# Rewriting a hybrid decoder layer so that attention, mLSTM and cross attention are emitted between the dense projections

## Chip, cores, metric

One Trainium2 chip, all 8 cores. Each core computes one of eight batch elements; nothing is exchanged between cores. The metric is device time in microseconds (us) of the slowest core.

In the calls of the experiments, 11 of 12 fast executions of the kernel before took 3553 to 3564 us, a spread of 0.3%; the twelfth took 3604. Other executions were in a slower state, in which the cores of one die (0 to 3, or 4 to 7) show a lower granted TensorE clock than the others: one of the kernel before took 3843 us, with a mean clock of 0.83 on one die and 0.91 on the other. No slow execution was profiled. Where a profile was taken on one core, the text names it if it matters.

Engine names: PE is TensorE (matmul), PEld its weight load, DVE is VectorE, ACT is ScalarE, POOL is GpSimd, SP is the sync engine, whose queue issues most loads and stores here. In these programs every matmul writes a bank of PSUM; to evacuate a bank is to move its result on to SBUF, the on-chip memory, so that the program can use the bank again. Tile names in the views: `bk` is a PSUM bank, `mv`, `mg` and `mb` are a chunk's values, gates and decays, `Cf` is the recurrent state of the mLSTM, `hmt` its output after the root, `Pa` the exponentials of attention, `hb` the inputs of the merge.

## The reference, cut to what matters

```python
# B=8, S=2048, D=2048; weights and shapes cut
def reference(x, mem, positions, ...):
    h = rms_norm(x, norm)
    proj = h @ w_in            # qk 2048, v 1024, o 1024, z 1024, gates i,f; cq 512, ckv 512, kr 64, az 1024; c_q 1024, c_z 1024; merge gates 3*2048
    # A: mLSTM, 4 heads of 256
    qk = silu(causal_depthwise_conv(m_qk, conv_w, conv_b))       # 4 taps
    hm = mlstm_chunkwise(q, k, v, ig, lf)                        # recurrent over chunks
    hm = rms_norm(hm) * sigmoid(m_o) * silu(m_z)
    # B: latent attention, 8 heads, causal, rotary part from cos/sin of the positions
    ha = causal_block_attention(qa, ka, v_a) * silu(a_z)
    # C: cross attention, 4 heads of 256, 256 memory tokens
    hc = memory_attention(c_q, k_mem, v_mem) * silu(c_z)
    # merge
    merged = sigmoid(g_m) * (hm @ w_br_m) + sigmoid(g_a) * (ha @ w_br_a) + sigmoid(g_c) * (hc @ w_br_c)
    return rms_norm(x + merged @ w_out, final_norm)
```

## The kernel before

It runs stage after stage, with barriers between: input projections, memory projections, cross attention, latent attention, mLSTM, then twice (for each half of the tokens) merge and output. A helper inserts every semaphore wait from declared reads and writes; each engine then takes its own instructions in the order in which the program emitted them. The two mLSTM parts:

```python
# mLSTM, two heads at a time; everything of a head is loaded once for all 16 chunks
fw.dma("sp", Brs[i]..., BHv[h:h + 1, :].partition_broadcast(128), ...)   # cumulated log decays, 1 MB once per head
fw.op("act", ... EBs = exp(Brs));  fw.op("dve", ... BMs = Brs + Mneg)    # whole rows, once
def P1a(c): ...   # scores q.k of chunk c, decay weights DT = exp(BM + At), PT = scores * DT, weighted keys kw
def P1b(c): ...   # state update Cf = decay * Cf + kw.v through a PSUM bank; bf16 copy Cb
def P2a(c): ...   # output bank = qe.Cb + PT.v
def P2b(c, bos):  # normalisation: 2 DVE and 2 ACT operations
    ...tensor_scalar(max 1, *EPS) ; scalar_tensor_tensor(...)            # DVE
    activation(Ln) ; activation(Exp, scale=-0.5)                         # ACT: x ** -0.5
    ...
P1a(0); P1b(0); P1a(1); P1b(1)
for c in range(16):
    if c + 2 < 16: P1a(c + 2)
    # (cut)
```

In the qk projection a block of 2048 tokens is evacuated to SBUF, then convolved with four long DVE operations, and its SiLU is one ACT operation.

The softmax here doesn't subtract the row's maximum and nothing guards it: scores larger than these inputs give would overflow.

## Time and profile before

| | before |
|---|---|
| median, first 3 runs | 3566.68 us (3559.03 to 4069.53, the last one slow) |
| profiled execution, slowest core (6) | 3566.3 us |

The first lines of the profile page of the kernel before: the span, busy time by engine, and, in 40 equal slices of the span, the busy tenths of PE and DVE and the granted TensorE clock in tenths.

```profile
span 3566.3 us, 43630 instructions; the slowest of 8 cores (3506.5 to 3566.3 us)
PE 2956.1 (83%) x14733; PEld 1383.4 (39%) x14733; DVE 912.9 (26%) x1781; ACT 847.2 (24%) x1783; POOL 272.9 (8%) x374
PE   1899999899999993667772524799999779999978
DVE  2556333311000450422222524011111221111113
PEclk9999999999999996978885555899999889999989
```

PE is full in the projections and in merge and output, and starved from slice 16 to slice 25 (counted from 1): memory projections, the two attentions and the mLSTM, each alone. In the mLSTM (slices 22 to 25) PE is 2 to 5 tenths busy and its clock is 0.5.

The windows view of the kernel before gives sums for a stretch; columns are the window, its length, then busy us (and instruction count) of PE, PEld, DVE, ACT, POOL, then the granted clock, the DMA share, GB/s. The lines are attention, the mLSTM of two heads, and part of the merge.

```profile
1545.00:1900.00 355.00, 265.93 (x1785) 129.98 (x1783) 78.31 (x365) 180.89 (x340) 4.75 (x16) 0.85 0.21 53
1900.00:2060.00 160.00, 61.62 (x340) 34.80 (x340) 66.14 (x188) 66.29 (x224) 25.28 (x60) 0.50 0.30 93
2262.00:2755.00 493.00, 492.48 (x2272) 222.60 (x2270) 62.43 (x95) 51.02 (x94) 94.03 (x92) 1.00 0.41 84
```

The merge is at its limit: 492 of 493 us busy at clock 1.00. The mLSTM of all four heads takes 315 us (1900 to 2215) for about 123 us of PE at a granted clock of 0.50.

### The profile page before, as it was taken

Reading aid. Unit: us, or ns where it says so; the run is one execution under the profiler, and the core shown is the slowest. Engines: PE = TensorE matmul, PEld = TensorE weight load, DVE = VectorE, ACT = ScalarE, POOL = GpSimd, SP = SyncE. Lnnn points to the kernel's source line nnn. Section 1 sums busy time; section 2 is a strip of 40 time slices with the busy share of each in tenths; the row PEclk is TensorE's granted clock in tenths of the full one; section 3 lists DMA queues with packets and bytes.
Section 4 is the critical chain, followed back from the end, with each engine's and each line's share of the span. In section 5 each row is a group of like instructions: output and inputs, shape, how many; then the busy total and the mean of one; then the engine's idle time right before and its main releaser. Section 6 shows DMA issues by size and latency. Waiting matters only on the chain.

```text
span 3566.3 us, 43630 instructions; the slowest of 8 cores (3506.5 to 3566.3 us)
## 1 busy us (share of the span) xinstructions
PE 2956.1 (83%) x14733; PEld 1383.4 (39%) x14733; DVE 912.9 (26%) x1781; ACT 847.2 (24%) x1783; POOL 272.9 (8%) x374
## 2 busy tenths in 40 slices
PE   1899999899999993667772524799999779999978
PEld 1444444444444442333331212344444334444433
DVE  2556333311000450422222524011111221111113
ACT  3432211232101121445552524001110110101111
POOL 0000000000000000000001111021222002221100
PEclk9999999999999996978885555899999889999989
DMA  8542330313232247332214051644434763333633
GB/s 211 177 92 68 86 74 21 68 25 61 65 80 54 71 129 181 110 89 66 66 39 125 20 170 43 144 80 80 80 73 88 180 219 77 70 71 76 127 95 142
DMA packets 139608, 338.15 MB, mean 95 GB/s; under 512 B 42048, under 2 KB 91520, under 8 KB 124160
## 3 DMA queue, kind: packets, MB, share of 16 engines
q0 software_dynamic: 15264, 143.24, 22.1%
q1 hardware_dynamic: 124128, 192.13, 16.7%
q8 instruction: 124, 2.03, 0.2%
q14 instruction: 92, 0.75, 0.1%
HBM read 396.47 MB, written 82.08 MB: 134 GB/s over the span
## 4 chain that ended last, share of the span: by engine, by line
PE 75%; DMA 8%; ACT 5%; issue 4%; DVE 4%; SPq 2%; another core or an unknown queue 0%; DVEq 0%; POOL 0%; ACTq 0%; POOLq 0%
PE bk L315 20%; PE bk L1018 18%; PE bk L304 13%; PE bk L1023 9%; PE bk L1062 6%; SPq L93 2%; PE bk L761 2%; ACT sb_Pa L746 2%; DMA sb_wpo<-wOUT 2%; DMA sb_hb<-HMT 2%; PE bk L741 1%; PE bk L743 1%; DMA sb_rn_xt<-mem 1%; DMA sb_rn_xt<-x 1%; ACT sb_rn_junk L234 1%
## 5 line engine op out<-in xcount | busy, mean ns | idle before, releaser
L1018 PE MATMUL bk<-sb_hTh,sb_wpg 128*128 128x512 bf16 x3072 | 682.8, 381 | 36.5 <-DMA sb_wpg<-wG 25.4
L315 PE MATMUL bk<-sb_wpA,sb_hT 128*128 128x512 bf16 (+1 forms) x3328 | 687.5, 367 | 8.2 <-DVE sb_stA L471 8.2
L1018 PEld LDWEIGHTS bk<-sb_hTh,sb_wpg 128*128 128x128 bf16 x3072 | 301.4, 98 | 402.3 <-issue 42.7
L315 PEld LDWEIGHTS bk<-sb_wpA,sb_hT 128*128 128x128 bf16 x3328 | 309.6, 99 | 373.0 <-issue 34.1
L1023 PE MATMUL bk<-sb_hb,sb_wpb 128*128 128x512 bf16 x1536 | 351.1, 382 | 26.4 <-DMA sb_hb<-HMT 26.4
L304 PE MATMUL bk<-sb_hT,sb_wpA 128*128 128x512 bf16 (+1 forms) x1664 | 367.9, 385 | 2.3 <-issue 2.3
L1029 ACT ACTIVATE sb_sg<-bk 128x512 f32<-128x512 f32 x192 | 104.2, 595 | 900.2 <-PE bk L1018 871.5
L304 PEld LDWEIGHTS bk<-sb_hT,sb_wpA 128*128 128x128 bf16 (+1 forms) x1664 | 166.1, 100 | 203.3 <-issue 23.9
L1023 PEld LDWEIGHTS bk<-sb_hb,sb_wpb 128*128 128x128 bf16 x1536 | 151.1, 98 | 211.1 <-issue 32.6
L1035 DVE TENSOR_TENSOR sb_tmpc<-sb_sg,bk 128x512 f32<-128x512 f32 x128 | 82.4, 684 | 576.5 <-PE bk L1023 576.5
L746 ACT ACTIVATE sb_Pa<-bk 128x512 bf16<-128x512 f32 (+1 forms) x320 | 169.8, 533 | 155.6 <-PE bk L761 54.3
L761 PE MATMUL bk<-sb_vx,sb_Pa 128*128 128x129 bf16 x1088 | 126.3, 237 | 53.4 <-DVE sb_Pa L748 28.1
L1062 PE MATMUL bk<-sb_wpo,sb_mergedT 128*128 128x512 bf16 x512 | 121.8, 398 | 33.0 <-DMA sb_wpo<-wOUT 33.0
L761 PEld LDWEIGHTS bk<-sb_vx,sb_Pa 128*128 128x128 bf16 x1088 | 80.3, 105 | 167.7 <-issue 160.0
L257 PE MATMUL bk<-sb_identb,sb_rn_xb 128*128 128x128 bf16 x288 | 33.6, 309 | 134.6 <-DVE sb_rn_xb L246 134.6
L741 PE MATMUL bk<-sb_qn,sb_kn 128*128 128x512 bf16 (+1 forms) x320 | 126.8, 396 | 16.8 <-DMA sb_kn<-KNT 15.8
L1031 DVE TENSOR_TENSOR sb_acc<-sb_sg,bk 128x512 f32<-128x512 f32 x64 | 44.0, 688 | 360.4 <-PE bk L1023 356.7
L743 PE MATMUL bk<-sb_qr,sb_kr 128*128 128x512 bf16 (+1 forms) x320 | 127.2, 398 | 0.0
L1038 POOL TENSOR_TENSOR sb_acc<-sb_acc,sb_tmpc 128x512 f32<-128x512 f32 x64 | 80.7, 1261 | 601.8 <-DVE sb_tmpc L1035 597.2
L1062 PE MATMUL bk<-sb_wpoa,sb_mergedT 128*128 128x512 bf16 x512 | 118.9, 393 | 8.0 <-POOL sb_mergedT L1041 8.0
L876 PE MATMUL bk<-sb_mqT,sb_mkT 128*128 128x128 bf16 x128 | 25.2, 300 | 119.7 <-DMA sb_mkT<-MKT 74.7
L531 DVE CAST sb_ob<-bk 128x512 bf16<-128x512 f32 x48 | 32.9, 689 | 349.1 <-ACT sb_ob L529 345.0
(227 smaller groups left out, 2408.4 us busy)
## 6 DMA issues: line engine op xcount, KB each, us to landing
sb_wpg<-wG POOLq DMA_DIRECT2D x32, 1536.0 KB, 10.4
sb_wpA<-wA POOLq DMA_DIRECT2D x18, 2048.0 KB, 16.1
sb_wpb<-wBR POOLq DMA_DIRECT2D x32, 768.0 KB, 13.5
sb_rn_xt<-x SPq DMA_DIRECT2D x16, 1024.0 KB, 6.6
sb_xo<-x SPq DMA_DIRECT2D x16, 1024.0 KB, 7.8
out<-sb_xo SPq DMA_DIRECT2D x16, 1024.0 KB, 4.8
HT<-sb_hT SPq DMA_DIRECT2D x16, 512.0 KB, 2.7
sb_wpM<-wMEM POOLq DMA_DIRECT2D x4, 2048.0 KB, 21.0
```

The lines of the kernel that those rows point to most:

```text
L304: fw.op("pe", lambda e: e.matmul(bk[0:M, 0:n], lhsT=wv[:, kc, c0:c0 + M], rhs=src[:, kc, tb * 512:tb * 512 + n], start=(kc == 0), stop=(kc ...
L315: fw.op("pe", lambda e: e.matmul(bk[:, 0:ncols], lhsT=src[:, kc, tt * 128:(tt + 1) * 128], rhs=wv[:, kc, 0:ncols], start=(kc == 0), stop=( ...
L741: fw.op("pe", lambda e: e.matmul(bs[:, 0:ncols], lhsT=kn[:, kc_], rhs=qn[:, q0:q0 + ncols], start=True, stop=False), reads=[r_kn, r_qn], w ...
L743: fw.op("pe", lambda e: e.matmul(bs[:, 0:ncols], lhsT=kr[:, kc_], rhs=qr[:, q0:q0 + ncols], start=False, stop=True), reads=[r_kr, r_qr], w ...
L746: fw.op("act", lambda e: e.activation(out=P[:, 0:ncols], in_=bs[:, 0:ncols], func=AF.Exp, scale=SC), reads=[r_bs], writes=[r_P])
L761: fw.op("pe", lambda e: e.matmul(bo[:, 0:129], lhsT=P[:, j * 128:(j + 1) * 128], rhs=vx[:, kt, 0:129], start=(kt == 0), stop=(kt == qt)), ...
L1018: fw.op("pe", lambda e: e.matmul(gb[tb][0][:, 0:512], lhsT=wgv[:, kc, b * 128:(b + 1) * 128], rhs=hTh[:, kc, tb * 512:(tb + 1) * 512], sta ...
L1023: fw.op("pe", lambda e: e.matmul(rb[tb][0][:, 0:512], lhsT=wbv[:, kc, b * 128:(b + 1) * 128], rhs=hbs[b][:, kc, tb * 512:(tb + 1) * 512], ...
L1029: fw.op("act", lambda e: e.activation(out=sg[:], in_=gb[tb][0][:, 0:512], func=AF.Sigmoid), reads=[gb[tb][1]], writes=[r_sg])
L1035: fw.op("dve", lambda e: e.tensor_tensor(out=tmp[:], in0=sg[:], in1=rb[tb][0][:, 0:512], op=ALU.mult), reads=[r_sg, rb[tb][1]], writes=[r_ ...
L1038: fw.op("pool", lambda e: e.tensor_tensor(out=acc[:, tc_], in0=acc[:, tc_], in1=tmp[:], op=ALU.add), reads=[r_tmp, r_acc], writes=[r_acc])
L1062: fw.op("pe", lambda e: e.matmul(bk[:, 0:512], lhsT=mergedT[:, kc, t8 * 128:(t8 + 1) * 128], rhs=wov[:, kc, 0:512], start=(kc == 0), stop= ...
```

## The change

The intent: give PE dense matmuls while attention, mLSTM and cross attention wait. The program is rewritten around Python generators. `dense_all` yields after each piece of projection; a scheduler then advances the current side job as long as its estimated PE work is below 0.36 of the dense work. Latent attention goes beside the az, qk and v projections and the beginning of oz, the mLSTM beside cq/cz, cross attention beside the first seven gate units of the merge. The diff has 2,400 lines; its core (all cuts marked):

```diff
+        sides = [(mla_gen, "MLA", 0.36), (mlstm_gen, "ML", 0.36), (c_gen, "CC", 0.36)]
+        for v in dense_all():
+            ...
+            st["d"] += v
+            while st["s"] < st["ratio"] * st["d"] and side_step():
+                pass
@@ PSUM: dense work has two banks, the side job six
+            misc, bub, bob = Ring(SB[0:2]), Ring(SB[2:4]), Ring(SB[4:6])
@@ attention, feature-major: up to 512 columns a matmul, softmax sums on DVE, reciprocal through DRAM
-    matmul(bo[:, 0:129], lhsT=P[:, j*128:(j+1)*128], rhs=vx[:, kt, 0:129])        # one per query tile
+    mm(po, (…, slice(512 - n, 512)), vx[:, kt, :], p[:, 0:n])
+    tt("dve", acc[:, o:512], acc[:, o:512], p[:, 0:n], ALU.add)
@@ convolution of one 512-token bank at a time, gate by tanh
+    copy("act", p[:, 3:515], bk[:, 0:512])
+    ts("dve", y, p[:, 3:515], cw[3], cb) ; 3 x stt("dve", y, p[:, tap:tap + 512], cw[tap], y)
-    activation(out=ob, in_=ybuf, func=AF.Silu)
+    act(th, y, AF.Tanh, scale=0.5) ; stt("dve", o, th, 1.0, y, ALU.add, ALU.mult) ; store
@@ mLSTM: all four heads a chunk, decays loaded chunk by chunk, root by Newton steps on DVE
+    B2s = tiles("mb", 2, [128, 4, 128], F32)
+    def loads1(c): mv, mg, and  dma(B2s[c % 2], BHv[:, chunk c].partition_broadcast(128))
+    def P1a(c): act(EB, B2, Exp) ; tt("dve", BM, B2, Mneg) ; ... DT = exp(BM), PT, kw
+    def rsqrt(y, x, t): shift, subtract, 3 x (mult, mult, mult-add, mult)          # DVE, [128, 2]
+    for c in range(16):
+        P1a(c + 1) ; P1b(c, 4 heads) ; P2(c, 0) ; P2(c, 1) ; tail(c - 1)
+        loads1(c + 2)
@@ tables for the rotary part: full width, one quarter of the tokens in one go, in the c_q projection
@@ one output phase at the end (before: twice merge then output)
```

## The prediction

> **What bounds it now.** TensorE. The engine table gives PE 2956 of 3566 us busy; the chain of waits is 75% PE. A dense 128x512 matmul starts every 215.9 ns (chain of waits: 32 in 6.91 us) at a granted clock of 1.00 (windows view): dense stages are at their limit. Counted in such matmuls, the program is about 12,400, 2680 us. In the other 890 us PE waits or runs slow. By stage (windows view; PE work my count):
>
> - start, norm of x: 120 us, PE 30 busy
> - input projections: 1226 for about 1185
> - memory projections and cross attention: 199 for 65
> - attention: 355 for 176; PE waits for ACT's exp (533 ns mean) and DVE's mask
> - mLSTM: 315 for 64, granted clock 0.50
> - merge and output: 1351 for 1216, with 135 of waits for hb, wOUT and first weights at stage edges
>
> [...] all eight cores hold 1.00 in the merge.
>
> **What changes.** Attention goes beside the az, qk, v and oz projections, mLSTM beside cq/cz, cross attention beside seven prepaid gate units. PE work falls little: feature-major attention replaces 1088 x 129 columns by 320 matmuls of up to 512, rope projections shrink (UQ 384 to 256, KR 128 to 64). My count is 12,270 matmuls, 2650 us, plus 30 for float32 denominators. Barriers, the hT round trip and the second output-weight load go. [...]
>
> **What stays or is added** (estimates from durations in the groups view):
>
> - Start: x arrives at 3.4 to 5 us a tile; PE fills from 40 us: 55.
> - Trig on DVE (about 10 us a quarter), uq weights: 20.
> - Memory projections stay exposed: four 2 MB loads at 16 to 21 us through two buffers against 7 us of matmul each: 45.
> - qk with attention is DVE-bound: per unit one 0.38 and four 0.684 us operations, plus 1.9 us of softmax sums, masks and scaling, 5.1 against 4.7 us of PE: 35 over 64 units.
> - Attention denominators: PE waits for DVE sum, then reciprocal, 32 times about 1.5 us: 45.
> - mLSTM: DVE about 16.5 us a chunk (two reciprocal roots, each 14 dependent 0.165 us operations) against 15 of PE, and only two output banks: 65.
> - Cross attention partly runs alone, then hb2 and branch weights load: 35.
> - Tail: 10.
>
> 2680 + 310 = 2990; some waits overlap, so I say **2960 us, 2850 to 3080** (8 in 10). Faster by over 2% 0.97, within 2% 0.02, slower 0.01.
>
> **What would show it.** PE busy above 90%; granted clock near 1.00 during mLSTM; no slice with PE at 2 to 5 tenths after the start except the memory projections (waiting for wMEM) and the cross-attention tail; DVE over 90% busy in the qk stretch, PE waits there and in mLSTM released by DVE; the merge still 10.4 us per gate-branch unit, without 30 us gaps for hb or wOUT; dense matmuls still 215.9 ns apart.
>
> **What would make it wrong.** [...] An in-order DVE or SP queue, waiting on the reciprocal's DRAM round trip, could hold back evacuations. If interleaving hides DVE chains better than I think, 2850.

(Three passages, two on the granted clock and one on the tables of ACT, are cut from the prediction, since they rested on no trace or run of this case. No term of the sum goes with them: it came to 2680 us of PE work, 2650 plus 30, and 310 of waits, 2990 in all, put at 2960 for overlap. What was measured: in the merge of the kernel before, from 2400 to 2600 us, all eight cores were granted 1.00. The kernel after shows no table load on ACT from 509 to 1573 us, with tanh and exponentials side by side in the qk stretch; a table load takes 1.28 us there. The 30 us for float32 denominators were an estimate; the 256 matmuls for them were busy 37 us in the kernel after.)

## The result

| | before | after |
|---|---|---|
| median | 3571.99 us (4 runs) | 3721.02 us (4 runs, 3692.53 to 3993.81) |
| ratio of fast runs | 1 | 1.0375 (95%: 1.0331 to 1.0419) |
| control, another chip | 3559 to 3563 us | 3625.18 us, its only fast run |

A ratio is the mean time of one kernel's fast runs over that of the other's fast runs of the same rounds, so it is not quite the ratio of the medians.

The kernel is slower. In the two runs behind the 1.0375, cores 6 and 7 ended at 3686 to 3700 us with a clock of 0.89, while the other six ended at 3597 to 3629 us with 0.90 to 0.91. They count as fast, but in the control no core of the fast run ended after 3625 us, and all clocks were 0.90 to 0.91. I take 3625 us, 1.018 of the control's fast before runs, as the undisturbed size, and use the control for sums by stage. Either way the predicted 2960 us is missed by over 660 us.

The answering lines of the page of the kernel after (core 6, the late one), with the first line of its chain of waits, which names what the chain that ended last consisted of:

```profile
span 3699.6 us, 41439 instructions; the slowest of 8 cores (3597.0 to 3699.6 us)
PE 2875.4 (78%) x13618; PEld 1367.3 (37%) x13885; DVE 1295.0 (35%) x2738; ACT 761.1 (21%) x1509; POOL 341.2 (9%) x410
PE   3679569877779999944444446748999999999998
DVE  3535214567674455423333333131111111111143
PEclk9889789989899999977777678969999999999999
PE 60%; DMA 15%; DVE 13%; issue 6%; ACT 4%; SPq 2%; DVEq 1%; ACTq 0%; POOLq 0%
```

The hole of before has not closed. From slice 18 to slice 24 PE is 4 tenths busy at 0.6 to 0.7 clock, although dense work was available all that time. The chain of waits went from 75% PE and 8% DMA to 60% PE and 15% DMA.

The windows view of the kernel after, the same core: start, qk with attention, cq/cz with mLSTM, the end of cross attention, part of the merge.

```profile
0.00:280.00 280.00, 159.07 (x890) 82.31 (x906) 109.24 (x143) 117.87 (x257) 5.10 (x13) 0.85 0.33 90
660.00:1128.00 468.00, 353.67 (x1523) 163.00 (x1553) 321.15 (x602) 124.93 (x252) 2.64 (x5) 0.89 0.24 62
1570.00:2287.00 717.00, 318.80 (x1492) 152.01 (x1520) 245.75 (x888) 139.37 (x325) 36.32 (x33) 0.72 0.25 53
2330.00:2520.00 190.00, 112.42 (x524) 47.70 (x533) 52.43 (x101) 27.19 (x47) 11.00 (x18) 0.75 0.69 159
2520.00:2962.00 442.00, 439.86 (x2004) 199.87 (x2044) 62.55 (x91) 48.95 (x82) 120.60 (x147) 1.00 0.50 83
```

The merge is as full as before. In the mLSTM stretch of 717 us no engine is busy for half the time. So it is not a matter of work but of waiting. The waits view of that stretch (engine, instruction, what it waited for: us in total, times, longest):

```profile
PE bk L289 <- DVE Cf_13317 L309: 280.7, 57, 23.5
DVE BM_127_13307 L302 <- DMA mb_121_13301<-BH: 133.1, 8, 29.0
DVE BM_127_13307 L302 <- DMA mb_122_13302<-BH: 123.0, 8, 19.1
```

PE waited 281 us for the state update on DVE. DVE waited 256 us, 16 us in each of 16 chunks, for one load: `mb`, the decays of the chunk, broadcast to all partitions. One chunk in the timeline of the kernel after (start us, duration, engine, instruction, in brackets the idle time before it and what ended it):

```profile
1908.74 0.44 SPq L132 DMA_DIRECT2D mb_121_13301<-BH  x1
...
1922.38 0.69 DVE L302 TENSOR_TENSOR BM_127_13307<-mb_121_13301,Mneg_13243 128x512 f32<-128x512 f32 x1 [15.32 <-DMA mb_121_13301<-BH]
1923.14 2.46 POOL L302 TENSOR_TENSOR qe_134_13314<-mq_111_13291,EB_126_13306 128x512 bf16<-128x512 bf16 x2 [42.22 <-ACT EB_126_13306 L293]
...
1928.11 0.37 PE L289 MATMUL bk<-mv_116_13296,kw_136_13316 128*128 128x257 bf16 x1 [18.79 <-DVE Cf_13317 L309]
```

The load is issued at 1908.74, behind those of `mv` and `mg`. Its data is there at 1922.4. The very next DVE instruction of the program reads it. The reason is in the loop: `loads1(c + 2)` stands at the end of iteration c, and iteration c + 1 begins with `P1a(c + 2)`. Nothing lies between. The buffer had been free for nearly two chunks, since only `P1a(c)`, at the start of iteration c - 1, reads it (in this trace at 1827.8); the place in the program alone makes the load late. DVE and ACT stand at it for 15.3 and 18.3 us, and the evacuation of a dense bank, which is emitted later, stands behind it: the last matmuls into that bank ended at 1909.1, but it was first read at 1924.95. PE had by then used both banks of the state update for two matmuls at 1908.93; the next one needs a bank that DVE has to free, and PE stops for 18.8 us. The next load of `mb` is issued at 1952.5, so a chunk took 44 us.

### The profile page after: what moved, and what is told of

The parts are those of the page before. It is cut to its first block, busy times and chain, and to the rows that moved or that the text cites. A ratio compares the mean times of both kernels' runs of the same rounds, so it can differ in the third digit from the quotient of the medians.

```text
span 3699.6 us, 41439 instructions; the slowest of 8 cores (3597.0 to 3699.6 us)
## 1 busy us (share of the span) xinstructions
PE 2875.4 (78%) x13618; PEld 1367.3 (37%) x13885; DVE 1295.0 (35%) x2738; ACT 761.1 (21%) x1509; POOL 341.2 (9%) x410
## 4 chain that ended last, share of the span: by engine, by line
PE 60%; DMA 15%; DVE 13%; issue 6%; ACT 4%; SPq 2%; DVEq 1%; ACTq 0%; POOLq 0%
PE bk L289 59%; DMA mb_122_13302<-BH 4%; DMA mb_121_13301<-BH 3%; DVE y_100_5053 L309 2%; DVE y_101_5054 L309 2%; SPq L132 2%; DMA hb_193_19251<-HCT 1%; DVE den_80_3545 L302 1%; DMA xt_14_61<-x 1%; DMA xo_209_26268<-x 1%; DMA cq_170_18127<-CQT 1%; DVE Cf_13317 L309 1%; DVEq L71 1%; DMA RDC<-rtc_184_18141 1%; ACT DT_128_13308 L293 1%
## 5 line engine op out<-in xcount | busy, mean ns | idle before, releaser
L289 PE MATMUL bk<-hT_10_52,w_12_54 128*128 128x512 bf16 x622 | 180.2, 440 | 4.3 <-issue 2.4
L289 PE MATMUL bk<-hT_9_51,w_11_53 128*128 128x512 bf16 x657 | 173.5, 415 | 11.5 <-DMA w_11_53<-wA 7.7
L289 PE MATMUL bk<-hT_10_52,w_11_53 128*128 128x512 bf16 x653 | 168.1, 406 | 3.6 <-DVE e_3_47_3200 L309 1.9
L289 PE MATMUL bk<-hT_9_51,w_12_54 128*128 128x512 bf16 x623 | 162.2, 406 | 1.2 <-issue 0.4
L289 PE MATMUL bk<-w_11_53,hT_9_51 128*128 128x512 bf16 (+1 forms) x630 | 132.5, 363 | 19.0 <-ACT hT_9_51 L297 6.7
L289 PE MATMUL bk<-w_11_53,hT_10_52 128*128 128x512 bf16 (+1 forms) x629 | 134.6, 367 | 5.2 <-ACT hT_10_52 L297 4.8
L289 PE MATMUL bk<-hT_9_51,wg_153_18094 128*128 128x512 bf16 x503 | 116.4, 386 | 8.4 <-DMA wg_153_18094<-wGB 7.9
L289 PE MATMUL bk<-hT_9_51,wg_155_18096 128*128 128x512 bf16 x502 | 112.9, 379 | 0.5
L289 PE MATMUL bk<-hT_9_51,wg_154_18095 128*128 128x512 bf16 x502 | 112.8, 379 | 0.5
L289 PE MATMUL bk<-hT_10_52,wg_155_18096 128*128 128x512 bf16 x502 | 112.6, 379 | 0.5
L289 PE MATMUL bk<-hT_10_52,wg_154_18095 128*128 128x512 bf16 x502 | 112.4, 379 | 0.5
L289 PE MATMUL bk<-hT_10_52,wg_153_18094 128*128 128x512 bf16 x502 | 112.4, 379 | 0.5
L289 PE MATMUL bk<-w_12_54,hT_9_51 128*128 128x512 bf16 (+1 forms) x501 | 110.5, 365 | 0.7 <-issue 0.2
L289 PE MATMUL bk<-w_12_54,hT_10_52 128*128 128x512 bf16 (+1 forms) x503 | 109.0, 362 | 0.4
L309 DVE SCALAR_TENSOR_TENSOR tm_198_19257<-sg_158_18099,bk 128x512 f32<-128x512 f32 x31 | 21.3, 687 | 246.8 <-PE bk L289 246.8
L289 PEld LDWEIGHTS bk<-hT_9_51,w_11_53 128*128 128x128 bf16 x672 | 70.1, 105 | 97.1 <-issue 35.6
L309 DVE SCALAR_TENSOR_TENSOR tm_198_19257<-sg_156_18097,bk 128x512 f32<-128x512 f32 x30 | 20.6, 688 | 239.4 <-PE bk L289 239.4
L289 PEld LDWEIGHTS bk<-hT_10_52,w_12_54 128*128 128x128 bf16 x640 | 70.6, 111 | 89.6 <-issue 38.0
L289 PEld LDWEIGHTS bk<-hT_10_52,w_11_53 128*128 128x128 bf16 x672 | 69.1, 103 | 85.9 <-issue 19.7
L293 ACT ACTIVATE sg_156_18097<-bk 128x512 f32<-128x512 f32 x46 | 27.5, 597 | 342.0 <-PE bk L289 342.0
L289 PEld LDWEIGHTS bk<-hT_9_51,w_12_54 128*128 128x128 bf16 x640 | 65.6, 104 | 77.1 <-issue 17.8
L289 PEld LDWEIGHTS bk<-w_11_53,hT_9_51 128*128 128x128 bf16 x640 | 63.7, 100 | 81.3 <-issue 28.0
```

Of the source, the lines that this page charges most:

```text
L289: fw.op("pe", lambda e: e.matmul(bk[o] if not isinstance(o, bass.AP) else o, lhsT=lhsT, rhs=rhs, start=start, stop=stop), reads=reads, wri ...
L293: fw.op("act", lambda e: e.activation(out=out, in_=in_, func=func, **kw), reads=reads, writes=writes, accs=accs)
L309: fw.op("dve", lambda e: e.scalar_tensor_tensor(out=out, in0=in0, scalar=sc, in1=in1, op0=op0, op1=op1), reads=reads, writes=writes, accs= ...
```

## The experiments

My theory A after reading the trace: the just-in-time load, passed on by in-order engines, is the largest loss, and smaller losses of the same kind (a wait at the head of an in-order list) account for most of the rest. Rivals: B, too few PSUM banks; C, interleaving itself costs more than it brings; D, the DVE has too much work. (The expectations use letters of their own in places: "theory C" in e3_conv and e4_serial is the in-order coupling, which here belongs to A; "rival E" in e4_serial is C here; rival B of e1_mb and e6_mbring takes in the DVE's chain of operations.) Eleven runs, all correct; one of them is the unchanged kernel as a control. Sums by stage are taken from the timeline, as the time between the first stores of successive stages: the qk stretch from the first store of q to that of v, the mLSTM stretch from the first store of cq to that of `RDC` (the reciprocals of cross attention). The control ran on another chip than e1_mb to e4_serial.

### e1_mb and e2_ring: the load, or the banks

```diff
# e1_mb: a third buffer, and the load issued one chunk earlier
-B2s = tiles("mb", 2, ...)            # loaded in loads1(c), c % 2
+B2s = tiles("mb", 3, ...)            # loadsB(c), c % 3
+                loadsB(c + 3)         # after loads1(c + 2)
# e2_ring: four banks shared instead of two and two
-misc, bub, bob = Ring(SB[0:2]), Ring(SB[2:4]), Ring(SB[4:6])
+misc, bub = Ring(SB[0:2]), Ring(SB[2:6]); bob = bub
```

> The changed kernel with one thing different: the row-broadcast load of the decay sums (mb<-BH) has a third buffer and is issued one whole chunk earlier; everything else is as changed. Theory A (the mLSTM stretch, 717 us on core 6, is set by this load, issued right before the DVE and ACT instructions that need it, some 14 to 19 us of wait in each of 16 chunks, and everything behind them on the in-order DVE waits too): the stretch falls by 240 to 300 us to about 440, the kernel to about 3440 us (ratio to before 0.96 to 0.975). Rival B (the stretch is set by the DVE chain of the reciprocal roots and the two output banks): the wait only changes its name; less than 80 us gained, ratio above 1.015.

> The changed kernel with one thing different: in mLSTM, the two banks of the state update and the two banks of the output form one ring of four, so that the second pair of heads need not wait for the first pair's root chain; the load of the decay sums stays just in time. Theory A: the waits of PE for these banks (about 75 us for hmt and part of those for Cf) shrink, the load's wait stays: 60 to 110 us gained, ratio 1.01 to 1.02. Rival B: the larger part of the stretch's excess of about 360 us goes, over 200 us, ratio below 0.985.

Measured: e1_mb 3479.84 us median, fast runs 3477 to 3480, ratio 0.9754 (0.9671 to 0.9837). One load issued a chunk earlier makes the rewrite faster than the kernel before, though the interval doesn't clear 2%, so the verdict on record is "unclear". (By the order of reads the third buffer would not even be needed for that; without it nothing was run.) The mLSTM stretch fell from 713 us (control) to 559: 154 us, nearly twice what rival B allowed, but well short of the 240 to 300 that theory A had expected. e2_ring: 3604.40 us, ratio 1.0087 (0.9989 to 1.0186), stretch 665 us: 48 us, below theory A's 60 to 110 and far from rival B's 200. In e2_ring the waits for the load are all still there. The waits views of the mLSTM stretches, first of the control, then of e2_ring, then of e1_mb:

```profile
PE bk L289 <- DVE Cf L309: 220.3, 56, 18.8
DVE BM L302 <- DMA mb<-BH: 190.6, 16, 29.1
PE bk L289 <- DVE hmt L309: 76.8, 17, 6.2
```

```profile
DVE BM L302 <- DMA mb<-BH: 193.6, 16, 29.6
PE bk L289 <- DVE Cf L309: 151.4, 35, 20.2
```

```profile
PE bk L289 <- DVE hmt L309: 78.8, 17, 6.0
PE bk L289 <- DVE Cf L309: 58.9, 56, 6.8
```

In e1_mb the load does not appear among the leading waits (2 waits of DVE, 25 us in all, are left), and PE's wait for `Cf` fell from 220 us (control) to 59. The wait for `hmt` stayed as it was, 77 us before and 79 after, and now leads. Theory A holds for the largest single part, not for the size it had claimed; banks alone explain at most 48 us.

### e3_conv: order in the qk unit

```diff
-act(th, y, AF.Tanh, scale=0.5); stt("dve", o, th, 1.0, y, ...); store
+def fin_(...): act(th, ...); stt(o, ...); store
+if cfin[0] is not None: cfin[0]()      # the unit before
+cfin[0] = fin_
```

> The changed kernel with one thing different: in the qk projection the tanh, the final product and the store of a unit are emitted behind the convolution of the next unit, instead of right behind their own. Theory C (the qk stretch, 468 us for 301 us of PE work, is a coupling of two in-order queues: ACT waits for the convolution on DVE with the softmax exponentials queued behind it, and DVE then waits for the tanh): 60 to 110 us gained, ratio 1.01 to 1.022. Rival D (DVE is simply full there): under 25 us, ratio 1.03 or more.

Here it is ACT's order that counts. Its tanh waits for DVE's four convolution operations (4.22 us below), and the exponentials of attention, emitted later, stand behind the tanh. From the timeline of the kernel after in the qk stretch, and from the waits view of ACT there (the first of six such lines, 299 us in all):

```profile
809.76 2.46 DVE L309 SCALAR_TENSOR_TENSOR y_100_5053<-pre_97_5050,cw_5044,y_100_5053 128x512 f32<-128x512 f32 x3
812.32 0.63 ACT L293 ACTIVATE e_2_52_3205<-y_100_5053 128x512 f32<-128x512 f32 x1 [4.22 <-DVE y_100_5053 L309]
813.13 0.69 DVE L309 SCALAR_TENSOR_TENSOR e_2_46_3199<-e_2_52_3205,y_100_5053 128x512 bf16<-128x512 f32 x1 [0.90 <-ACT e_2_52_3205 L293]
```

```profile
ACT e_2_52_3205 L293 <- DVE y_100_5053 L309: 57.9, 11, 10.9
```

Measured: 3588.73 us median of 5, two of them slow; fast 3565 to 3589; ratio 1.0018 (0.9924 to 1.0112), a little better than the range that the coupling had been given. The qk stretch fell from 444 us (control) to 384, with the same operations in it. ACT's wait for `y`, control first, then e3_conv:

```profile
ACT e L293 <- DVE y L309: 291.9, 63, 8.3
```

```profile
ACT e L293 <- DVE y L309: 61.1, 37, 4.0
```

PE's waits for `Pa` fell with it, from 86 to 38 us. Emitting three instructions later was worth 60 us, the lower end of the 60 to 110 expected.

### e4_serial: is interleaving a loss?

```diff
-sides = [(mla_gen, "MLA", 0.36), (mlstm_gen, "ML", 0.36), (c_gen, "CC", 0.36)]
+sides = [(mla_gen, "MLA", 1e6), (mlstm_gen, "ML", 1e6), (c_gen, "CC", 1e6)]
```

> The changed kernel with the interleaving off: each of the three side programs is emitted in one piece when its inputs are ready (the ratio of side to dense work set to a million). Theory A and C (the interleaving itself helps, what costs are single waits within it): slower than the changed kernel by 60 to 250 us, ratio 1.055 to 1.11. Rival E (putting small work between the dense matmuls, with two banks left to the dense ones, is what costs): faster than the changed kernel by 50 us or more, ratio below 1.02.

Measured: 3748.92 and 3752.61 us (the median of 3890 us holds two slow runs), 1.052 of the fast before runs, just under the range expected. Interleaving is a gain of some 125 us over the whole, so rival C falls as stated. By stage it is split, though. At the first oz store interleaving is 172 us ahead (1287 us against 1459), but there the serial kernel is done with attention (last store at 1022 us), while the interleaved one still carries the end of it through oz (to 1521). The fair mark is the first store of `BH`, with which the mLSTM begins: 1579 against 1679, a gain of 101 us with latent attention. From there to the start of cross attention, the mLSTM with its projections, interleaving gains only 13 us (712 against 724). With one late load per chunk, overlapping the two was worth hardly more than running them after one another. The serial run also shows the new mLSTM by itself, in the windows view, and below it, from the waits view, how long DVE waited for the load of `mb` there:

```profile
1691.00:2130.00 439.00, 112.23 (x630) 68.39 (x630) 216.20 (x752) 108.94 (x263) 34.77 (x30) 0.53 0.27 54
```

```profile
DVE BM L302 <- DMA mb<-BH: 80.9, 8, 28.9
```

439 us alone, where that of the kernel before took 315. DVE waited 81 us of it for the same load, in 8 of the 16 chunks (191 us in all 16 in the control). Even less these 81 us (an estimate: 358) it is the slower of the two: the rewrite brought a slower mLSTM and counted on hiding it. Alone and without the late load it was not run.

### e5_control, e6_mbring, e7_all, e8_best

```diff
# e6_mbring = e1_mb + e2_ring
# e7_all    = e6 + e3_conv + two more:
#   tables: the operations of a quarter go into a list; five of them after each projection unit
-                        trig_step()          # a whole quarter, after each of the first four c_q units
+                    trig_step(5)
#   cross attention: side work at 0.8 instead of 0.36 of dense work, hb loads ahead of the seven gate units
# e8_best   = e7 + one root for all four heads of a chunk, 11 DVE operations instead of 2 x 17
-rsqrt(sc[:, 8:10], ...)   twice a chunk, three Newton steps of 4 operations
+2 Newton steps of 3:  u = y*y ; u = u*x ; y = (u - 3) * y ; then (u - 12) * y    # constants folded into the scale
```

> The changed kernel again, untouched, as the control of this call. Expected 3610 to 3720 us, 1.015 to 1.04 of the kernel before. In its first runs two cores of one die (6 and 7) ended at 3690 us while the other six ended at 3597 to 3629 us: if that was a state of that chip or of that run, this one comes out near 3620 us; if it belongs to the kernel (cores 6 and 7 always late), near 3700 us.

> The broadcast load one chunk earlier AND a four-bank ring shared by state update and output. Theory A (in the changed kernel the load hid the two-bank ring: the ring alone gave nothing because DVE and ScalarE stood at the load): with the load out of the way the ring is worth something, about 60 us: the mLSTM stretch about 500 us, the total about 3420 us, ratio 0.955 to 0.97. Rival B (with the load early, the stretch is held by the DVE's in-order list itself, whatever the number of banks): no more than the early load alone, 3470 to 3490 us, ratio 0.975, and the waits of TensorE for the state copies simply move to another tile.

> Five repairs together: load early, four-bank ring, gate of each qk unit behind the next convolution, the sine and cosine work spread five operations at a time, and cross attention with its loads ahead of its gate units and at 0.8 instead of 0.36 of side work to dense work. If the losses add up: about 3210 us, ratio 0.895 to 0.915. Rival: the losses hide behind each other, since the later stages wait for the stage before on the same DVE, and less than half of the sum arrives: 3300 us or more.

> The five repairs and a shorter reciprocal square root of the mLSTM output: one for all four heads of a chunk with two Newton steps, about 10 dependent DVE operations a chunk in place of two chains of 17. At the 0.267 us from start to start that such operations showed this saves about 6 us of DVE a chunk. Theory A (the DVE's in-order list is what holds the mLSTM stretch once the load is early): the stretch is 16 x 5 to 6 us = 80 to 95 us shorter than with the five repairs, total about 3120 us. Rival B (the stretch is held by TensorE or by loads): under 20 us less.

| run | fast runs, us | ratio (95%) | to first kr store | qk | cq/cz with mLSTM | cross attention to end |
|---|---|---|---|---|---|---|
| e5_control | 3625.18 | 1.018, one run | 293 | 444 | 713 | 1334 |
| e6_mbring | 3442 to 3472 | 0.9691 (0.963 to 0.9751) | 293 | 446 | 523 | 1368 |
| e7_all | 3342 to 3345 | 0.9389 (0.937 to 0.9407) | 260 | 383 | 524 | 1329 |
| e8_best | 3254 to 3260 | 0.9145 (0.9124 to 0.9166) | 258 | 382 | 445 | 1324 |

The columns of a row come from its profiled run; that of e6_mbring (3471.66 us) was the slowest of its fast ones, its last column above that of the others.

In e6_mbring the ring is worth 36 us in its stretch after the load was moved (559 to 523 us), against 48 us before; in total ratio it brings 0.6%. The ratio is inside theory A's range, at its upper end; the stretch gained 36 us where about 60 had been expected. So the ring is worth something with the load early, but not more than with it late: that the load had hidden the ring's worth, as the expectation said, is not borne out. Rival B's "no more than the early load alone" falls (3442 to 3472 us against e1_mb's 3477 to 3480).

In e7_all the gains of stages add up: 33 (start) + 61 (qk) + 189 (mLSTM) + 5 (cross attention to end) = 288 us, where the profiled spans of control and e7 differ by 283 us (3624.1 to 3341.4). But the total of 3343 us misses the expected 3210; it lies in the range that the rival had named (3300 or more), though the rival's reason, losses that hide behind each other, is not what the sums show: more than half of the expected gain arrived, and the single gains had been set too high. Of the two parts not tried alone, spreading the table work brought 33 us, and the cross-attention repair 5 us, in the sum of its stretch to the end. The waits views of PE up to the first kr store, control first, then e7_all, show the table work: in the control PE stands behind whole quarters of up to 12.5 us, since a projection's evacuation waits behind them on DVE.

```profile
PE bk L525 <- DVE c L309: 50.3, 5, 12.5
```

```profile
PE bk L525 <- DVE c L309: 19.9, 9, 3.2
```

In e8_best the mLSTM stretch falls by 79 us, 4.9 us in each of 16 chunks, with 23 DVE operations a chunk fewer. That is just under the 80 to 95 us expected; the total misses the expected 3120 by as much as e7_all had missed its own. The windows views of the stretch, e7_all first, then e8_best:

```profile
1489.00:2012.00 523.00, 342.31 (x1727) 164.78 (x1726) 267.74 (x889) 144.00 (x338) 38.28 (x35) 0.83 0.37 90
```

```profile
1490.00:1935.00 445.00, 323.35 (x1696) 161.65 (x1729) 198.23 (x522) 145.50 (x338) 38.91 (x35) 0.86 0.45 106
```

The operations are tiny, [128, 2]. Four of them in the timeline of the kernel after:

```profile
1901.48 0.17 DVE L320 TENSOR_SCALAR stm_150_13330<-stm_150_13330 128x2 int32<-128x2 int32 x1
...
1901.76 0.17 DVE L321 TENSOR_SCALAR stm_150_13330<-stm_150_13330 128x2 int32<-128x2 int32 x1
...
1902.03 0.16 DVE L323 TENSOR_TENSOR stm_150_13330<-stm_150_13330 128x2 f32<-128x2 f32 x1
...
1902.30 0.16 DVE L324 TENSOR_TENSOR stm_150_13330<-stm_150_13330 128x2 f32<-128x2 f32 x1
```

Each lasts 0.165 us, but they start 0.27 us apart. 23 x 0.27 = 6.2 us of DVE a chunk, of which 4.9 arrived. (The root now also comes once, after all four heads; that change of order is in the 4.9 too.) Planning with the duration alone, as the prediction did, undercounts such a chain by 40%.

### e9_order, e10_tap, e11_last

```diff
# e9_order, on e8_best: mq/mk loads one chunk earlier; reciprocal's load one step later
-                if c % 2 == 1 and c // 2 + 2 < 8: loads(c // 2 + 2)
+                if c % 2 == 0 and c // 2 + 2 < 8: loads(c // 2 + 2)
-                dma(rb, RDC ...)      # right after the store to RDC
+                rbl[0] = rbl_         # issued in the next step, behind its loads
# e10_tap, on e8_best: first convolution tap on ACT, from the bank
-ts("dve", y, p[:, 3:515], cw[3], cb, mult, add)
+act(y, bk[:, 0:512], AF.Identity, scale=cw[3], bias=cb)
# e11_last = e9 + e10 + softmax sums on POOL
-tt("dve", acc[:, o:512], acc[:, o:512], p[:, 0:n], ALU.add)
+tt("pool", ...)
```

> The kernel of e8_best with two changes of the order in which loads are given to the queue, no work added or removed. In the mLSTM the loads of q and k for the next pair of chunks are issued one chunk earlier (their buffers are free by then). In cross attention the load that brings the reciprocals back is issued one step later, behind the loads of the next step, because in e8_best the queue stood 64 us for 16 such round trips and the next step's cq came late (PE waited 38 us for mk and 38 us for cq there). Theory: each wait shows in its own stretch: mLSTM 445 to about 415 us, cross attention 134 to about 110 us, total 3200 to 3215 us against 3254. Rival (TensorE would have waited for the next thing in those places): under 15 us in all.

> The kernel of e8_best with the first tap of the convolution of the qk stretch on ScalarE (scale and bias read from the bank), 64 operations of about 0.57 us off the DVE. Theory (the qk stretch, 382 us in e8_best, is held by the DVE, busy 306 us of it, TensorE work in it 321 us at a clock of 0.91): DVE falls by about 35 us, the stretch by 20 to 35 us, to about 350 us. Rival (it is held by the order of hand-overs between ScalarE and DVE): no gain, 375 us or more, since a hand-over is added.

> All repairs together: e9_order, e10_tap, and the adds of the softmax sums that are still on the DVE given to POOL where the tile is a whole one. If gains of different stretches add: about 3160 us, 0.885 to 0.895 of the kernel before. The adds on POOL alone are open: by the DVE theory they bring the qk stretch 10 to 25 us further down than e10_tap; the rival is that POOL is slower for such an add and TensorE waits for the sums instead, then the stretch is as long as in e10_tap or longer.

| run | fast runs, us | ratio (95%) | qk | cq/cz with mLSTM | cross attention to merge loads |
|---|---|---|---|---|---|
| e8_best | 3254 to 3260 | 0.9145 (0.9124 to 0.9166) | 382 | 445 | 134 |
| e9_order | 3270 to 3273 | 0.9194 (0.9157 to 0.9231) | 382 | 441 | 147 |
| e10_tap | 3227 | 0.9069 (0.9006 to 0.9131) | 341 | 447 | 137 |
| e11_last | 3241 to 3249 | 0.9117 (0.9072 to 0.9161) | 350 | 441 | 152 |

(The last column runs from the first store of `RDC` to the load of the cross-attention output for the merge.) e9_order is a miss: 3270 us where 3200 to 3215 were expected, a little slower than e8_best. In the mLSTM PE's wait for `mk` fell from 38 to 14 us, but its wait for `Cf` rose from 22 to 39, and 4 us were gained. In cross attention it got worse by 13 us. The waits of the SP queue there, e8_best first, then e9_order:

```profile
SPq L71 <- DMA RDC<-rtc: 64.2, 16, 7.1
```

```profile
SPq L71 <- DVE hc L302: 92.4, 31, 8.5
```

The round trip of the reciprocal left the queue, and a wait for the stores of `hc` took its place, since DVE, which makes `hc`, now waited longer for the reciprocals to come back: 71 us in 16 waits, against 23 us in 7. Theory A's rule, that each wait shows in its own stretch, does not hold for these two: removing the one that is listed let another one appear in the same place.

e10_tap is the best kernel: 3227 us, 0.907 of the kernel before. DVE work moved to ACT shortens the qk stretch by 41 us, where 20 to 35 had been expected. So there, once the order is repaired, the stretch follows the DVE's work, as the prediction held. (The first tap also no longer waits for ACT's copy of the bank; what that shorter chain adds was not separated.) The windows views of the qk stretch, e8_best first, then e10_tap:

```profile
665.00:1047.00 382.00, 321.20 (x1441) 153.14 (x1469) 305.54 (x582) 124.67 (x238) 2.11 (x4) 0.91 0.28 71
```

```profile
667.00:1008.00 341.00, 309.37 (x1455) 146.71 (x1455) 270.72 (x519) 165.29 (x299) 2.15 (x4) 0.94 0.31 78
```

DVE falls by 35 us, the stretch by 41 us, and PE ends 91% busy in it. e11_last takes DVE down by a further 25 us there (273.64 to 248.89 us over 345 us), and the stretch gets 9 us longer, not shorter, with 113 us of POOL in it: 100 instructions more than in e10_tap took 111 us on POOL, 1.11 us each, and in the kernel after a 128x512 float32 add took 1.26 us on POOL (in the merge) against 0.69 on DVE (in the softmax sums). The rival of the expectation held, a stretch no shorter than in e10_tap. Whether the DVE still limits past e10_tap this run doesn't tell, since the slower adds came with it. With e9_order in it too, the total of 3241 to 3249 us misses the expected 3160.

## Why the prediction was wrong

The step that failed is the term "mLSTM: DVE about 16.5 us a chunk ... against 15 of PE, and only two output banks: 65". The amount of DVE work was about right: DVE was busy 252 us in the control's mLSTM stretch, 15.8 us a chunk. But a chunk took 44 us. I had compared sums of work, as if engines that are each below their limit would overlap, and never asked in which order each in-order engine meets its waits. The program text has the answer: a load issued at the end of an iteration is read by the first instruction of the next. The dense projections of that stretch need about 221 us (1024 matmuls at 215.9 ns; the oz projection of equal size, with nothing beside it in e4_serial, took 221 us), the mLSTM about 64 us by my count, together some 285 us. Measured were 713 us. So the term is about 430 us instead of 65. (The expectation for e2_ring has 360: it took 290 us for the dense part, the time of oz in the control, but there the end of attention runs beside it.) By the experiments, 154 us of that are the load (e1_mb), 36 more the shared banks (e6_mbring), 79 more the count of small operations (e8_best). The remaining 160 us, 445 against 285, were not taken apart; e9_order's attempt on them gave 4 us.

Other points:

- **"qk with attention is DVE-bound ... 35".** With 4.7 us of PE for each of 64 units, 301 us, the control's 444 us are a loss of about 140 us. 60 us were ACT's tanh standing in front of exponentials (e3_conv), 41 us were DVE work (e10_tap), some 40 stay open. The mechanism I named was there, but the larger part was order, and it hid the other: at 321 of 468 us DVE was 69% busy, not over 90%.
- **Start and trig, "55" and "20".** The first kr store came at 293 us. PE was busy 159 us before 280 at clock 0.85, about 135 us at full clock (an estimate, busy time times clock), so about 145 us were lost against 75. 33 us come from the undivided table work (e7_all). The rest was not tested.
- **Cross attention, "35".** In the stretch 2330 to 2520 PE was busy 112 of 190 us at 0.75; by the same estimate about 105 us were lost. PE's longest waits there are for the loads of cq, 40 us in all. Two attempts at the stage (in e7_all and e9_order) brought 5 us and cost 13. What bounds it stays open.
- **Memory projections, "45".** On core 6, 400 to 505 us, PE was busy 50 of 105 us at 0.74: about 68 us lost. Not tested.
- **Granted clock "near 1.00 during mLSTM".** 0.72. That the clock would be near 1.00 was my estimate; the kernel before shows 1.00 where PE was busy 492 of 493 us (merge) and 0.50 where it was busy 123 of 315 (mLSTM). PE waited 57 times for `Cf` here, 281 us in all and up to 23.5 us at a time. When the waits shrank, the clock rose: 0.75 (control), 0.82 (e1_mb), 0.86 (e8_best). No run separates the clock from the waits, so what sets the clock was not shown.
- **Right:** the dense matmul and the merge. 1391 matmuls in 300 us of merge are 215.7 ns each at clock 1.00 on the fullest cores, with PE 440 of 442 us busy; all eight cores were granted 1.00 there, with PE busy 298 to 300 of the 300 us; no gap of 30 us for hb or wOUT came back. Latent attention beside projections was a gain of 101 us (e4_serial), which was the intent of the change.
- **What I named as a danger** was an "in-order DVE or SP queue, waiting on the reciprocal's DRAM round trip". The kind was right, the place wrong, and I gave it no weight: the chance of slower stood at 0.01, and the lower and upper bounds were made from sums of work.

In one sum: the control lost about 945 us against the 2680 us of PE work that I counted, where I had allowed 280. The repairs brought 398 us of that back (3625 to 3227); 267 us of the miss of 665 remain.

## What to carry to other kernels

When work of two kinds is interleaved on engines that take their instructions in emitted order, do not add up busy times (here they gave 65 us where 430 were lost): for each load and each hand-over, find the first instruction that reads it, and ask what stands behind that instruction on the same engine. Issue a load at least one whole iteration before its reader, with buffers enough for it: here one broadcast load of 256 KB, behind two other loads, took 13.6 us from issue to first use, and issuing it a chunk earlier turned 1.018 into 0.975. Then move operations that wait for another engine behind those that don't, cut the count of tiny dependent operations (23 fewer a chunk brought 4.9 us), and only then move work between engines (the first tap on ACT shortened the qk stretch by 41 us); and expect that one wait removed shows the next, as in e9_order.
